# Long raw and split tiles handed out by columns, and two own buffers for the conditioning rows, in a one-core encoder layer

## The chip, the cores and the metric

One Trainium2 chip, one core. The metric is device time in microseconds (us) of one execution; lower is better. The engines are TensorE (PE, with its weight loads shown as PEld), VectorE (DVE), ScalarE (ACT), GpSimd (POOL) and SyncE (SP), which issues most of the transfers. Each engine works through its own instructions in program order, and semaphores hold an instruction back until what it needs is there.

## The reference, cut to what matters

One encoder layer on x of 1024 tokens by 1024 channels, float32, with a conditioning vector c of 1024:

```
mod = silu(c) @ w_ada + b_ada            # 6 x 1024: shift, scale and gate for two halves
h   = rms_norm(x, g1) * (1 + scale) + shift
q, k, v, gates = h @ w_in                # 20 heads, 10 units of two heads, 384 columns a unit
a = neighbourhood attention (8 heads);  b = dilated windows (12 heads, 3 dilations)
y = merge of a @ w_proj_a and b @ w_proj_b by sigmoid gates
x = x + gate * (y @ w_o)
x = x + gate2 * SwiGLU(rms_norm(x, g2) modulated by the rest of mod)
```

All of it is float32 to the precision of a split product: each operand is cut into a high part and a low part, and three matmul passes (high by high, high by low, low by high) make one product.

## The kernel before, in words

**Start (until about 60 us).** x is loaded, transposed and normed. The conditioning vector's first two blocks of columns (2 x 1024) come in eight blocks of `land` tiles (two transfers of 512 KB each), and PE multiplies them with c block by block (`ada_rows`, L789). ACT copies the row out (`rowk`, L795), PE turns it into columns (L804), DVE finishes them (`sc`, L809 and L811) and scales `yT` (L816), ACT takes the high part of h (L821), DVE the low part (L824), and ACT sends `yT` off to `h_d` (L826, issued from ACT's own queue). The first unit's weights come in between (`raw`, 192 KB for 128 x 384 columns; ACT `whi` L118, DVE `wlo` L119), and PE multiplies block after block (`start_chunk`, L834).

**Units (60 to about 525 us).** Ten units u of two heads; six are dilated, four neighbourhood. A unit has 8 steps t of 128 tokens, and a step has 8 chunks k of three 384-column matmuls each (`proj_chunk`, L312). Step n is 8u + t. Between the chunks PE does the attention of earlier units. The weights of the next unit come by `unit_load` on SP (into 6 raw buffers of 512 columns), and `wsplit` makes the high part on ACT (L118) and the low part on POOL or DVE (L119), into 10 buffers of 512 columns: k = 0 and 1 in step 6, the other six within step 7's chunks, odd k on DVE. The norm of q and k (L330 to L335), their rotation (L342 to L345), the scaling after PE's turn (L377, then L400 to L402) and the softmax rows run on ACT, DVE and POOL.

**Conditioning rows in between.** The other 4096 columns of mod are made in 64 turns of `ada_step`: eight sums (`acc`, one buffer) of eight multiply-adds each on DVE (the first of a sum is L299, the other seven L301), whose 512 columns of w_ada stand in `wa` tiles. One transfer (L283) brings two turns' worth, 512 KB, into one of 8 large buffers shared with `land`, two turns ahead. `ada_row` sums a finished `acc` over the partitions on PE (L271) and writes the row (L274 to L276).

**What sets the order.** PE's order is written by hand for the whole kernel. In the start the other engines' order is written by hand too. Behind that, a scheduler orders ACT, DVE, POOL and SP by priorities and by when it takes buffers to come free. Loads and stores are told done on eight lanes (DMAHW0 to DMAHW7) that are used in turn, and an issue on a lane waits until the earlier one there has landed.

After the units come the gates, the merges, the output projection and the feed-forward part (to 1507 us), in which PE is the limit nearly throughout.

Of the kernel before, what the change touches and what calls it, by code (L numbers as in the profile page):

```python
# [23 lines left out]
NRAW, NHL = 6, 10  # L24
# [19 lines left out]
def hybrid_layer(ctx: ExitStack, tc: tile.TileContext, x, colp, wada1, wada2, bada2, wqkv, wg, wpa, wpb,  # L44
                 wo, w1, w2, hgain, ropeg, rope, rbias, bmask, g2r, out):
    nc = tc.nc

    def pool(name, side, **kw):
        return tc.alloc_tile_pool(name=name, bufs=1, side=side, reuse_waits="tile", **kw)
# [4 lines left out]
    wp = pool("w", "left")  # L54
# [6 lines left out]
    o_d = tc.dram_tile([6, 128, S], F32, name="o_d")  # L61
# [44 lines left out]
    def fview(ap):  # L106
        return ap.bitcast(F32)

    def wload(src, n):
        raw = wp.tile([128, 512], F32, tag="raw", bufs=NRAW, name="raw")  # L110
        nc.sync.dma_start(raw[:, :n], src)
        return raw[:, :n]

    def wsplit(r, eng=None):
        n = r.shape[1]
        hi = wp.tile([128, 512], F32R, tag="hi", bufs=NHL, name="whi")
        lo = wp.tile([128, 512], F32R, tag="lo", bufs=NHL, name="wlo")
        nc.scalar.activation(hi[:, :n], r, AF.Copy)  # L118
        (eng or nc.gpsimd).tensor_sub(lo[:, :n], r, fview(hi[:, :n]))  # L119
        return hi, lo  # L120

    def wslot(src, n):
# [20 lines left out]
    ap_ = pool("attn", "right")  # L143
# [2 lines left out]
    nc.vector.memset(c32, 0.0)  # L146
    nc.vector.tensor_copy(c32[:, :, 0], cact)

    NBIG, NLAND = 8, 7

    def big(name, shape=None, dtype=F32):
        return ap_.tile(shape or wide, dtype, tag="big", bufs=NBIG, name=name)
# [1 line left out]
    yT = [ap_.tile([128, 4, S], F32, tag="qk", bufs=2, name="yT") for _ in range(2)]  # L154
    land = [big("land") for _ in range(NLAND)]
    for tag, n, bufs in (("bm", 512, 1), ("p", 512, 4), ("qn", 256, 7), ("rtab", 512, 1), ("acc2", 512, 1), ("pT", 512, 4),
                         ("stg", 512, 3), ("vs", 128, 2), ("ra", 64, 2), ("rb", 64, 2)):
        ap_.tile([128, n], F32, tag=tag, bufs=bufs, name="place")
    seq = [0]

# [19 lines left out]
    def unit_load(u, k):  # L180
        return wload(wqkv[u, :, k, :], 384)
# [85 lines left out]
    ada_acc = {}  # L267

    def ada_row(c):
        pm = bank("t")  # L270
        nc.tensor.matmul(pm[0:1, :], ones, ada_acc[c], start=True, stop=True)  # L271
        row = wp.tile([1, 512], F32, tag="raw", bufs=NRAW, name="row")
        br = wp.tile([1, 512], F32, tag="raw", bufs=NRAW, name="brow")
        nc.sync.dma_start(br, bada2[:, c * 512:(c + 1) * 512])  # L274
        nc.vector.tensor_add(row, pm[0:1, :], br)
        nc.sync.dma_start(mod_d[c * 512:(c + 1) * 512].rearrange("(o n) -> o n", o=1), row)  # L276

    def ada_load(i):

        if i < 64 and i not in ada_acc.setdefault("w", {}):  # L280
            c, kk = divmod(i, 8)
            ada_acc["w"][i] = big("wa2", [128, 2, 512])
            nc.sync.dma_start(ada_acc["w"][i], wada2[c, :, kk:kk + 2, :])  # L283

    def ada_step():
        i = ada_state["i"]
        ada_state["i"] += 1
        c, kk = divmod(i, 8)
        if kk == 0 and c > 0:
            ada_row(c - 1)  # L290
        if i >= 64:
            return
        if kk % 2 == 0:
            ada_load(i)
            ada_load(i + 2)
        wa = ada_acc["w"][i - kk % 2][:, kk % 2, :]
        if kk == 0:
            ada_acc[c] = ap_.tile([128, 512], F32, tag="acc2", bufs=1, name="acc2")
            nc.vector.tensor_scalar(ada_acc[c], wa, cact[:, 0:1], None, op0=ALU.mult)  # L299
        else:  # L300
            nc.vector.scalar_tensor_tensor(ada_acc[c], wa, cact[:, kk:kk + 1], ada_acc[c],  # L301
                                           op0=ALU.mult, op1=ALU.add)
# [222 lines left out]
    class Cluster:  # L525


        def __init__(self):
            self.items, self.keys = [], 0
# [114 lines left out]
    def combine_prep(i):  # L644
        pr, g, hf = i // 6, (i % 6) // 2, i % 2
        if g == 0 and hf == 0:
            cb["acc"] = big("oacc")
        ut = wp.tile([128, 512], F32, tag="raw", bufs=NRAW, name="ut")
        u = u_d[g * 2 + pr]
        if g == 0:  # L650
            nc.sync.dma_start(ut, u[:, hf * 512:hf * 512 + 512])
            uv = ut
        elif g == 1:
            nc.sync.dma_start(ut.rearrange("p (r i) -> p r i", r=4),
                              u.rearrange("p (r h i) -> p h r i", r=4, h=2)[:, hf])
            uv = ut.rearrange("p (r i) -> p i r", r=4)
        else:
            nc.sync.dma_start(ut.rearrange("p (t i) -> p t i", t=8),
                              u.rearrange("p (t i) -> p t i", t=8)[:, :, hf * 64:hf * 64 + 64])
            uv = ut.rearrange("p (t i) -> p i t", t=8)  # L660
        fb = wp.tile([128, 4, 2, 64], F32, tag="raw", bufs=NRAW, name="fb")
        for hd in range(2):
            nc.vector.tensor_copy(fb[:, :, hd, :], cb["fe"][:, g, hf * 4:hf * 4 + 4, pr, hd, None]
                                  .to_broadcast([128, 4, 64]))
        cb[i] = (fb, ut, uv, cb["acc"])
# [254 lines left out]
    raws = {}  # L920
    nextw = {}
    for n in range(6, 92):
        u, t = divmod(n, 8)
# [7 lines left out]
        else:  # L931
            chunks = []
        if u + 1 < 10:
            for k in ([0, 1, 2, 3, 4, 5, 6, 7] if n == 6 else [t] if u else []):
                raws[u + 1, k] = unit_load(u + 1, k)
            if t == 6:
                for k in range(2):
                    nextw[u + 1, k] = wsplit(raws[u + 1, k])
        if t == 2 and 1 <= u <= 10:
            for slot, I in unit_items(units[u - 1]):  # L940
                if I.U.kind < 3:
# [19 lines left out]
        def chunk():  # L961
            if chunks:
                chunks.pop(0)()
                k = 8 - len(chunks)
                if t == 7 and u + 1 < 10 and k < 8 and k >= 2:
                    nextw[u + 1, k] = wsplit(raws[u + 1, k], nc.vector if k % 2 else None)

        turns = [(units[0], tt) for tt in {8: (0, 1), 9: (2, 3), 11: (4, 5), 13: (6, 7)}.get(n, ())]
        if PAIRED <= n <= 81 or 9 < n < PAIRED and n % 2:
# [56 lines left out]

    def gate_mixes(i, order):
        r = {q: gate_raw(i, q) for q in (0, 2, 3, 1)}
        s1 = wp.tile([128, 512], F32, tag="raw", bufs=NRAW, name="ws")
# [103 lines left out]
    def o_split():  # L1133
        for pr in (4, 5, 0, 1, 2, 3):
            oT[pr] = ttp.tile([128, 2, S], F32R, tag="t", bufs=6, name="oT")
            for hf in range(2):
                hs = slice(hf * 512, hf * 512 + 512)
                raw = wp.tile([128, 512], F32, tag="raw", bufs=NRAW, name="raw")
                nc.sync.dma_start(raw, o_d[pr][:, hs])
# [198 lines left out]
    def late_weights(j):  # L1338
        if j in EARLY[:2]:
            n = EARLY.index(j)  # L1340
            for nm, src in (("x2", w1_d[n, 1]), ("x3", w1_d[n, 2]), ("x1", w1_d[n, 0]), ("w22", w1[j, :, 12:16, :]),
                            ("x4", w1_d[n, 3])):
                wj[j, nm] = wsplit(wload(src, 512), nc.vector if n == 0 or nm in ("x3", "w22") else None)
            return
        r = {q: wload(w1[j, :, 4 * q:4 * q + 4, :], 512) for q in (0, 2, 3, 1)}
        s1, s2 = (wp.tile([128, 512], F32, tag="raw", bufs=NRAW, name="ws") for _ in range(2))
# [12 lines left out]
        nc.gpsimd.tensor_sub(s4, r[1], s4)  # L1359
        wj[j, "x4"] = wsplit(s4, nc.vector)  # L1360
# [305 lines left out]
```

## Time and profile before

| | |
|---|---|
| Runs | 1507.0, 1508.83, 1510.0 us; median 1508.83 |
| Profiled execution | 1508.52 us; its span, first to last instruction, 1506.7 us |
| PE busy | 1485.7 us, 99% of the span, 8156 matmuls |
| DVE busy | 1090.2 us (72%) |
| ACT busy | 668.2 us (44%) |
| POOL busy | 535.1 us (36%) |
| Mean granted TensorE clock | 0.999 |
| Transfers | 241.65 MB, 160 GB/s on average; 45.7% of 16 engines' span on the main queue |

How to read it: a row of the list of operations in time gives the start, the duration, the engine, the line, the operation with its output and inputs, and in brackets the idle time before it with what ended it. "PE ps_d L312 <- DVE wlo L119" in the list of waits means that PE's matmul of line 312 stood until DVE's operation of line 119 was done; the three numbers are the total in us, the count, and the longest. Matmuls overlap, so their pace is read from start to start (0.17 us for 384 columns) and not from their durations (0.33 us). PEclk is the granted clock, 1.00 being the full one.

### The profile page before, as it was taken

What the parts mean: (1) busy time and instruction counts of PE and PEld (TensorE: products, weight loads), DVE (VectorE), ACT (ScalarE), POOL (GpSimd) and SP (SyncE); (2) the same over time, 40 slices, a digit from 0 to 9 for tenths busy, and PEclk for the clock granted to TensorE, in tenths of its full rate; (3) what the DMA queues carried; (4) which work ended last, traced back from release to release, by engine and by line L of the source; (5) the groups of instructions that cost most, each with busy time, mean ns of one, the idle gap of its engine ahead of it and who ended that gap; (6) DMA issues with size and microseconds to landing.
All of it is one profiled execution on the core that took longest, in us unless ns stands there. A gap on an engine that the chain in (4) does not pass through costs nothing. (4 is left out here: it accounts for less than half of the span.)

```text
span 1506.7 us, 24201 instructions
## 1 busy us (share of the span) xinstructions
PE 1485.7 (99%) x8156; PEld 1265.1 (84%) x8156; DVE 1090.2 (72%) x2265; ACT 668.2 (44%) x1691; POOL 535.1 (36%) x540
## 2 busy tenths in 40 slices
PE   9999999999999999999999999999999999999998
PEld 7998989998888877788888888888888888887886
DVE  6867767767889845367675597788767777599468
ACT  5555655555645554246432354233223323354442
POOL 0432332321100040002352301676767776104464
PEclk9999999999999999999999999999999999999999
DMA  9625445645245164824553225345433334898342
GB/s 373 236 85 179 144 132 162 196 139 166 61 131 168 45 197 143 327 85 128 161 195 137 90 90 181 126 127 181 155 125 109 108 106 144 278 372 281 98 153 100
DMA packets 150637, 241.65 MB, mean 160 GB/s; under 512 B 26464, under 2 KB 69088, under 8 KB 149744
## 3 DMA queue, kind: packets, MB, share of 16 engines
q1 hardware_dynamic: 131936, 226.45, 45.7%
q10 hardware_dynamic: 18576, 13.64, 2.8%
q8 instruction: 65, 1.06, 0.3%
q14 instruction: 60, 0.49, 0.1%
HBM read 179.89 MB, written 60.15 MB: 159 GB/s over the span
## 5 line engine op out<-in xcount | busy, mean ns | idle before, releaser
L119 POOL TENSOR_TENSOR wlo<-raw,whi 128x512 fp32r<-128x512 f32 (+2 forms) x133 | 172.9, 1314 | 461.7 <-ACT whi L118 287.0
L118 ACT ACTIVATE whi<-raw 128x512 fp32r<-128x512 f32 (+1 forms) x348 | 203.6, 599 | 252.4 <-PE ps_s L1501 42.3
L312 PE MATMUL ps_d<-whi,hT 128*128 128x384 f32 x1152 | 310.8, 341 | 0.0
L119 DVE TENSOR_TENSOR wlo<-raw,whi 128x512 fp32r<-128x512 f32 (+1 forms) x215 | 183.6, 867 | 76.8 <-ACT whi L118 72.4
L312 PEld LDWEIGHTS ps_d<-whi,hT 128*128 128x128 f32 x1152 | 209.9, 188 | 5.2 <-ACT vs L350 3.5
L312 PE MATMUL ps_d<-wlo,hT 128*128 128x384 f32 x576 | 193.6, 336 | 2.9 <-DVE wlo L119 2.7
L312 PEld LDWEIGHTS ps_d<-wlo,hT 128*128 128x128 f32 x576 | 108.7, 189 | 4.0 <-DVE wlo L119 3.4
L118 ACT ACTIVATE whi<-ws 128x512 fp32r<-128x512 f32 x65 | 40.8, 628 | 126.9 <-DVE ws L1348 79.8
L1281 POOL TENSOR_TENSOR e<-e,c 128x512 f32<-128x512 f32 x44 | 68.9, 1565 | 59.2 <-DVE c L1411 35.0
L342 POOL TENSOR_TENSOR ra<-qn,rtab 128x64 f32<-128x64 f32 x48 | 16.3, 340 | 156.7 <-DVE qn L335 105.8
L119 POOL TENSOR_TENSOR wlo<-m,whi 128x512 fp32r<-128x512 f32 x35 | 51.4, 1479 | 54.5 <-ACT whi L118 54.5
L1279 ACT ACTIVATE e<-e 128x512 f32<-128x512 f32 x44 | 27.5, 631 | 95.1 <-DVE e L1414 66.4
L555 ACT ACTIVATE P<-P,st 128x256 f32<-128x256 f32 (+2 forms) x100 | 45.8, 460 | 41.4 <-DVE st L553 41.3
L712 PE MATMUL ps_d<-hT,whi 128*128 128x512 f32 x192 | 60.6, 397 | 0.0
L1331 PE MATMUL ps_v<-h2T,whi 128*128 128x512 f32 x192 | 59.2, 389 | 0.0
L1331 PE MATMUL ps_s<-h2T,whi 128*128 128x512 f32 x192 | 59.1, 389 | 0.0
L129 ACT ACTIVATE ry<-ss,eps 128x4 f32<-128x4 f32 (+1 forms) x88 | 26.2, 298 | 70.1 <-DVE ss L333 56.7
L1331 PE MATMUL ps_d<-h2T,whi 128*128 128x512 f32 x184 | 56.8, 390 | 0.0
L491 ACT ACTIVATE P<-P,sx 128x384 f32<-128x384 f32 (+1 forms) x64 | 37.1, 580 | 43.6 <-DVE sx L490 43.4
L119 DVE TENSOR_TENSOR wlo<-ws,whi 128x512 fp32r<-128x512 f32 x45 | 49.7, 1105 | 8.0 <-ACT whi L118 7.8
L1280 DVE TENSOR_TENSOR e<-e 128x512 f32<-128x512 f32 x44 | 42.5, 973 | 17.8 <-ACT e L1279 17.7
L301 DVE SCALAR_TENSOR_TENSOR acc<-wa,cact,acc 128x512 f32<-128x512 f32 x56 | 42.6, 762 | 16.8 <-DMA wa<-in_wada_dram 16.5
(445 smaller groups left out, 3956.8 us busy)
## 6 DMA issues: line engine op xcount, KB each, us to landing
raw<-in_w_dram SPq DMA_DIRECT2D x139, 256.0 KB
ga_d<-e SPq DMA_DIRECT2D x77, 256.0 KB
raw<-ga_d SPq DMA_DIRECT2D x77, 256.0 KB
wa<-in_wada_dram SPq DMA_DIRECT2D x32, 512.0 KB
raw<-in_wqkv_dram SPq DMA_DIRECT2D x80, 192.0 KB
m<-in_w_dram SPq DMA_DIRECT2D x44, 256.0 KB
raw<-in_wg_dram SPq DMA_DIRECT2D x42, 256.0 KB
xt<-in_x_dram SPq DMA_DIRECT2D x16, 512.0 KB
```

The costliest lines, as they stand in the source:

```text
L118: nc.scalar.activation(hi[:, :n], r, AF.Copy)
L119: (eng or nc.gpsimd).tensor_sub(lo[:, :n], r, fview(hi[:, :n]))
L129: nc.scalar.activation(y, ss, AF.Ln, scale=1.0 / n, bias=eps)
L301: nc.vector.scalar_tensor_tensor(ada_acc[c], wa, cact[:, kk:kk + 1], ada_acc[c], op0=ALU.mult, op1=ALU.add)
L312: nc.tensor.matmul(pd[:, :384], tok(a, k, t), U.w[k][b][:, :384], start=(k == 0 and i == 0), stop=(k == KT - 1 and i == 2))
L491: nc.scalar.activation(P[:nq, :nk], P[:nq, :nk], AF.Exp, scale=-1.0, bias=nm, accum_out=sm)
L555: nc.scalar.activation(C.P[h][:nq, c], C.P[h][:nq, c], AF.Exp, scale=-1.0, bias=nm, accum_out=sm)
L712: nc.tensor.matmul(st["p"], gw[i, br][j][a][:, kk * 128:(kk + 1) * 128], hT[b][:, k, hs], start=(k == 0 and q == 0), stop=(k == 7 and q == 2))
L1279: nc.scalar.activation(sg, a, AF.Sigmoid)
L1280: nc.vector.tensor_mul(sg, sg, a)
L1281: nc.gpsimd.tensor_mul(sg, sg, up)
L1331: nc.tensor.matmul(pb, w[p][:, k * 128:(k + 1) * 128], b[q][:, k], start=(k == 0 and i == 0), stop=(k == 3 and i == 2))
```

## The change

- **Ring.** The raw tile is one long tile of 3072 columns, and the high and low parts are two long tiles of 5120 columns. A `take(n)` hands out the next n columns and wraps round at the end. Unit weights take 384 columns each, so there are 8 raw slots and 13 slots for the parts, in the same memory that held 6 and 10 of 512. Elsewhere 512 columns are taken, on a multiple of 512, which gives 6 and 10 as before.
- **When weights are loaded and split.** From unit 1 on, the raws of the next unit are loaded one per step (two in step 6), and written as split one per step: k = 0 to 4 in steps 2 to 6, k = 5 to 7 behind the first three chunks of step 7. k = 1, 3 and 6 are on DVE.
- **Conditioning rows.** `wa` has two buffers of its own of 128 x 512. Each of the 64 turns has a transfer of 256 KB of its own, issued one turn ahead. The large buffers are 7 instead of 8. The row and its bias share one large buffer instead of two raw ones.
- `fb`, which held a raw buffer, takes one of the three `stg` buffers; `ut` and the feed-forward's sums take from the ring.

```
+    class Ring:
+        def __init__(self, n, dtype, name):
+            self.t, self.n, self.at = wp.tile([128, n], dtype, name=name), n, 0
+        def take(self, n, packed=False):
+            if n == 512 and not packed:
+                self.at = -(-self.at // 512) * 512
+            if self.at + n > self.n:
+                self.at = 0
+            self.at += n
+            return self.t[:, self.at - n:self.at]
+    rawr = Ring(NRAW * 512, F32, "raw")
+    hir, lor = Ring(NHL * 512, F32R, "whi"), Ring(NHL * 512, F32R, "wlo")
...
-    NBIG, NLAND = 8, 7
+    NBIG, NLAND = 7, 7
...
-            ada_acc["w"][i] = big("wa2", [128, 2, 512])
-            nc.sync.dma_start(ada_acc["w"][i], wada2[c, :, kk:kk + 2, :])
+            ada_acc["w"][i] = ap_.tile([128, 512], F32, tag="wa", bufs=2, name="wa2")
+            nc.sync.dma_start(ada_acc["w"][i], wada2[c, :, kk, :])
...
-        if kk % 2 == 0:
-            ada_load(i)
-            ada_load(i + 2)
-        wa = ada_acc["w"][i - kk % 2][:, kk % 2, :]
+        ada_load(i)
+        ada_load(i + 1)
+        wa = ada_acc["w"][i]
...
-        fb = wp.tile([128, 4, 2, 64], F32, tag="raw", bufs=NRAW, name="fb")
+        fb = ap_.tile([128, 4, 2, 64], F32, tag="stg", bufs=3, name="fb")
...
         if u + 1 < 10:
-            for k in ([0, 1, 2, 3, 4, 5, 6, 7] if n == 6 else [t] if u else []):
+            for k in (t - 2,) if 2 <= t < 7 and u else ():
+                nextw[u + 1, k] = wsplit(raws[u + 1, k], nc.vector if k in (1, 3) else None)
+            for k in range(5) if n == 6 else range(5, 8) if n == 7 else (6, 7) if t == 6 else (t,) if t < 6 else ():
                 raws[u + 1, k] = unit_load(u + 1, k)
-            if t == 6:
-                for k in range(2):
-                    nextw[u + 1, k] = wsplit(raws[u + 1, k])
+            for k in range(5) if n == 6 else ():
+                nextw[u + 1, k] = wsplit(raws[u + 1, k], nc.vector if k in (1, 3) else None)
...
-                if t == 7 and u + 1 < 10 and k < 8 and k >= 2:
-                    nextw[u + 1, k] = wsplit(raws[u + 1, k], nc.vector if k % 2 else None)
+                if t == 7 and u + 1 < 10 and k <= 3:
+                    nextw[u + 1, k + 4] = wsplit(raws[u + 1, k + 4], nc.vector if k == 2 else None)
```

The number of compute instructions is the same, and PE's rows are in the same order, one for one. SP has 32 rows more. Line numbers after the ring are higher by 15 or 16: L118 and L119 are now L134 and L135, L178 is L194, L283 is L299, L299 and L301 are L314 and L316, L826 is L841.

**SP in the start, behind the sixth `land` transfer.** `land` is half a block of conditioning columns, `raw` the first unit's weights, `wa_` the conditioning rows of the 64 turns. Before:

```order
L178 DMA land<-in_wada_dram 128x1024 [waits DMAHW5_49]
L178 DMA land<-in_wada_dram 128x1024 [waits DMAHW6_49,PE_49]
L111 DMA raw<-in_wqkv_dram 128x384 [waits DMAHW7_49]
L178 DMA land<-in_wada_dram 128x1024 [waits DMAHW0_49,PE_49]
L178 DMA land<-in_wada_dram 128x1024 [waits DMAHW1_49,PE_49]
L111 DMA raw<-in_wqkv_dram 128x384 [waits DMAHW2_49]
```

These are block 3's two halves, the fourth raw, block 4's two halves and the fifth raw. After, on the same engine and place:

```order
L194 DMA land<-in_wada_dram 128x1024 [waits DMAHW5_49]
L299 DMA wa_1057<-in_wada_dram 128x512 [waits DMAHW6_49]
L299 DMA wa_1059<-in_wada_dram 128x512 [waits DMAHW7_49]
L194 DMA land<-in_wada_dram 128x1024 [waits DMAHW0_49,PE_49]
L128 DMA raw<-in_wqkv_dram 128x384 [waits DMAHW1_49]
L194 DMA land<-in_wada_dram 128x1024 [waits DMAHW2_49,PE_49]
L194 DMA land<-in_wada_dram 128x1024 [waits DMAHW3_49,PE_49]
```

Two loads of conditioning rows, whose buffers are free from the beginning, now stand between the halves of block 3. Each later transfer here is on another lane than before.

**ACT and DVE in the start, at the second block of h.** ACT's rows before, from the first store of `yT` on:

```order
L826 DMA h_d<-yT 128x1024 [waits DMAHW7_49]
L118 ACTIVATE whi<-raw 128x384
L821 ACTIVATE hT_112<-yT 128x512 [waits DVE_49] x2
L826 DMA h_d<-yT 128x1024 [waits DMAHW1_49]
L795 ACTIVATE rowk<-ps_t 128x256 [waits PE_49]
```

ACT's rows after:

```order
L841 DMA h_d<-yT 128x1024 [waits DMAHW2_49]
L134 ACTIVATE whi<-raw 128x384 [waits DMAHW7_49]
L836 ACTIVATE hT_115<-yT 128x512 [waits DVE_49] x2
L841 DMA h_d<-yT 128x1024 [waits DMAHW4_49]
L810 ACTIVATE rowk<-ps_t 128x256 [waits PE_49]
```

The rows are the same, but the first store waits for the lane on which block 4's first half was put (before, the lane of the fourth raw). DVE's rows after, at the same block:

```order
L831 TENSOR_SCALAR yT<-yT,sc 128x512 [waits DVE_49]
L831 TENSOR_SCALAR yT<-yT,sc 128x512
L135 TENSOR_TENSOR wlo<-raw,whi 128x384 [waits DMAHW7_49,Activation_49]
L314 TENSOR_SCALAR acc_1061<-wa_1057,cact 128x512 [waits DMAHW6_49]
L839 TENSOR_TENSOR hT_405<-yT,hT_115 128x512 [waits Activation_49] x2
```

The row of `acc` between `wlo` and `hT` was not there before; the other four were. Six of the first sum's eight turns now stand in the start.

**DVE where unit 4 begins.** `tp` is a sum or difference of blocks of h that the gates will use later, `qk` the scaled and turned q and k, `wlo` a low part of weights. Before:

```order
L753 TENSOR_TENSOR tp<-tp 128x2x256 [waits DMAHW3_49,DMAHW2_49]
L754 TENSOR_TENSOR tp<-tp 128x256 [waits DVE_49]
L755 TENSOR_TENSOR tp<-tp 128x256 [waits DVE_49]
L401 SCALAR_TENSOR_TENSOR qk<-ps_v,hg,qk 128x4x64 [waits Activation_49]
L402 TENSOR_TENSOR qk<-ps_v,qk 128x4x64
L119 TENSOR_TENSOR wlo<-raw,whi 128x384 [waits DMAHW1_49,Activation_49]
```

After:

```order
L568 ISA P,st<-ps_s,bmask 128x256 [waits PE_49]
L568 ISA st 128x1
L350 TENSOR_TENSOR qn<-qn,ry 128x256 [waits DVE_49,Pool_49]
L568 ISA P,st<-ps_s,bmask 128x256
L568 ISA st 128x1
L590 COPY PT<-ps_t 128x512 [waits PE_49]
L416 SCALAR_TENSOR_TENSOR qk<-ps_v,hg,qk 128x4x64 [waits Activation_49]
L417 TENSOR_TENSOR qk<-ps_v,qk 128x4x64
L135 TENSOR_TENSOR wlo<-raw,whi 128x384 [waits Activation_49] x2
```

The three `tp` rows stand some thirty rows earlier, and two low parts follow `qk` where one did. All eight splits that a unit's time holds still stand in its step 7; of these, before, one or two were for the unit after next, and now four or five are.

More of the change, by code (lines that the diff above doesn't have):

```diff
@@ L107, in fview @@
         return ap.bitcast(F32)
+    class Ring:
[10 more added lines that the diff above has]
+    hir, lor = Ring(NHL * 512, F32R, "whi"), Ring(NHL * 512, F32R, "wlo")
     def wload(src, n):
-        raw = wp.tile([128, 512], F32, tag="raw", bufs=NRAW, name="raw")
-        nc.sync.dma_start(raw[:, :n], src)
-        return raw[:, :n]
+        raw = rawr.take(n if n == 384 else 512)[:, :n]
+        nc.sync.dma_start(raw, src)
+        return raw
     def wsplit(r, eng=None):
         n = r.shape[1]
[L116 to L119, printed above, removed]
+        hi, lo = (z.take(n if n == 384 else 512)[:, :n] for z in (hir, lor))
+        nc.scalar.activation(hi, r, AF.Copy)
+        (eng or nc.gpsimd).tensor_sub(lo, r, fview(hi))
         return hi, lo
@@ L156, in hybrid_layer @@
     for tag, n, bufs in (("bm", 512, 1), ("p", 512, 4), ("qn", 256, 7), ("rtab", 512, 1), ("acc2", 512, 1), ("pT", 512, 4),
-                         ("stg", 512, 3), ("vs", 128, 2), ("ra", 64, 2), ("rb", 64, 2)):
+                         ("stg", 512, 3), ("wa", 512, 2), ("vs", 128, 2), ("ra", 64, 2), ("rb", 64, 2)):
         ap_.tile([128, n], F32, tag=tag, bufs=bufs, name="place")
@@ L271, in ada_row @@
         nc.tensor.matmul(pm[0:1, :], ones, ada_acc[c], start=True, stop=True)
-        row = wp.tile([1, 512], F32, tag="raw", bufs=NRAW, name="row")
-        br = wp.tile([1, 512], F32, tag="raw", bufs=NRAW, name="brow")
+        z = big("row", [1, S])
+        row, br = z[:, 0:512], z[:, 512:1024]
         nc.sync.dma_start(br, bada2[:, c * 512:(c + 1) * 512])
@@ L647, in combine_prep @@
             cb["acc"] = big("oacc")
-        ut = wp.tile([128, 512], F32, tag="raw", bufs=NRAW, name="ut")
+        ut = rawr.take(512, True)
         u = u_d[g * 2 + pr]
@@ L1028, in gate_mixes @@
         r = {q: gate_raw(i, q) for q in (0, 2, 3, 1)}
-        s1 = wp.tile([128, 512], F32, tag="raw", bufs=NRAW, name="ws")
+        s1 = rawr.take(512)
         nc.vector.tensor_sub(r[0], r[0], r[2])
@@ L1137, in o_split @@
                 hs = slice(hf * 512, hf * 512 + 512)
-                raw = wp.tile([128, 512], F32, tag="raw", bufs=NRAW, name="raw")
-                nc.sync.dma_start(raw, o_d[pr][:, hs])
+                raw = wload(o_d[pr][:, hs], 512)
                 hi, lo = (oT[pr][:, b, hs] for b in range(2))
@@ L1345, in late_weights @@
         r = {q: wload(w1[j, :, 4 * q:4 * q + 4, :], 512) for q in (0, 2, 3, 1)}
-        s1, s2 = (wp.tile([128, 512], F32, tag="raw", bufs=NRAW, name="ws") for _ in range(2))
+        s1, s2 = rawr.take(512), rawr.take(512)
         nc.vector.tensor_add(s1, r[2], r[3])
```

## The prediction

> **What bounds the kernel now.** I read the page first, then what TensorE waited for, then the granted clock by stretches, and last the rows in time around the places that the change touches.
>
> ```profile
> span 1506.7 us, 24201 instructions
> PE 1485.7 (99%) x8156; PEld 1265.1 (84%) x8156; DVE 1090.2 (72%) x2265; ACT 668.2 (44%) x1691; POOL 535.1 (36%) x540
> ```
>
> TensorE is the bound: it stands idle for 1506.7 - 1485.7 = 21.0 us of the span, and since its own rows are the same, one for one, before and after, the change can win at most those 21 us and what a slow clock costs. So every part has to be priced in TensorE's waits. From the list of waits on TensorE, the two that name a split weight of the units:
>
> ```profile
> PE ps_d L312 <- DVE wlo L119: 2.7, 1, 2.7
> PE ps_d L312 <- POOL wlo L119: 0.2, 1, 0.2
> ```
>
> Nine unit boundaries, and only one long wait. Here it is in time, VectorE's rows and then TensorE's, and the stretches around it with the granted clock (the column behind POOL):
>
> ```profile
> 210.70 1.46 DVE L753 TENSOR_TENSOR tp<-tp 128x512 f32<-128x512 f32 x1 [2.05 <-DMA tp<-h_d]
> ...
> 214.77 0.41 DVE L402 TENSOR_TENSOR qk<-ps_v,qk 128x256 fp32r<-128x256 f32 x1
> 215.10 0.54 DVE L119 TENSOR_TENSOR wlo<-raw,whi 128x384 fp32r<-128x384 f32 x1
> ```
>
> ```profile
> 215.70 0.45 PE L312 MATMUL ps_d<-wlo,hT 128*128 128x384 f32 x1 [2.67 <-DVE wlo L119]
> ...
> 219.18 0.52 PE L312 MATMUL ps_d<-whi,hT 128*128 128x384 f32 x1
> 219.63 1.20 PE L543 MATMUL ps_s<-qk 64*128 64x256 f32 x12
> ```
>
> ```profile
> 205.00:215.00 10.00, 8.02 (x58) 7.53 (x56) 7.85 (x19) 6.00 (x19) 5.21 (x8) 1.00 0.65 204
> 215.00:220.00 5.00, 4.30 (x16) 3.87 (x18) 3.34 (x14) 1.72 (x7) 1.63 (x7) 0.67 0.22 66
> 220.00:225.00 5.00, 5.00 (x51) 4.69 (x50) 2.81 (x11) 3.67 (x13) 0.50 (x2) 0.99 0.11 27
> ```
>
> VectorE stood 2.05 us for a transfer of `tp`, did its `tp` rows, and only then the low part that TensorE needed at 213.0. Behind the wait the clock was granted at 0.67, and 14 matmuls took 219.63 - 215.70 = 3.93 us, where 14 at 0.173 us (the pace from start to start elsewhere in this loop) take 2.42: another 1.5 us.
>
> The second group are the waits for the conditioning rows. From VectorE's waits between 60 and 520 us, then five of the eight in time, and the TensorE rows that stand a little later:
>
> ```profile
> DVE acc L301 <- DMA wa<-in_wada_dram: 16.5, 8, 4.4
> ```
>
> ```profile
> 81.66 0.75 DVE L301 SCALAR_TENSOR_TENSOR acc<-wa,cact,acc 128x512 f32<-128x512 f32 x1 [1.47 <-DMA wa<-in_wada_dram]
> ...
> 140.89 0.75 DVE L301 SCALAR_TENSOR_TENSOR acc<-wa,cact,acc 128x512 f32<-128x512 f32 x1 [1.53 <-DMA wa<-in_wada_dram]
> ...
> 322.38 0.75 DVE L301 SCALAR_TENSOR_TENSOR acc<-wa,cact,acc 128x512 f32<-128x512 f32 x1 [4.36 <-DMA wa<-in_wada_dram]
> ...
> 367.13 0.75 DVE L301 SCALAR_TENSOR_TENSOR acc<-wa,cact,acc 128x512 f32<-128x512 f32 x1 [2.78 <-DMA wa<-in_wada_dram]
> ...
> 418.31 0.75 DVE L301 SCALAR_TENSOR_TENSOR acc<-wa,cact,acc 128x512 f32<-128x512 f32 x1 [3.41 <-DMA wa<-in_wada_dram]
> ```
>
> ```profile
> 86.14 0.44 PE L377 MATMUL ps_v<-ident,qn 128*128 128x128 f32 x2 [1.22 <-DVE rz L132]
> ...
> 146.00 0.44 PE L377 MATMUL ps_v<-ident,qn 128*128 128x128 f32 x2 [1.30 <-POOL qn L345]
> ...
> 369.02 0.50 PE L476 MATMUL ps_s<-qk 64*128 64x256 f32 x4 [0.95 <-DVE qk L402]
> ...
> 421.14 0.66 PE L672 MATMUL ps_t<-ident,fb 128*128 128x128 f32 x4 [0.98 <-DVE PT L506]
> ```
>
> No TensorE row names `wa`, but VectorE's loss of 1.5 to 3.4 us comes 2 to 5 us before four of TensorE's waits; that the one causes the other is my reading. The longest of all, 4.36 us at 322, is followed by none. TensorE lost 1.22 + 1.30 + 0.95 + 0.98 = 4.45 us for 16.5 us of VectorE: 0.27 us for each.
>
> **The change part by part.** The sum is against the profiled execution, 1508.52 us, which is 0.3 below the median of the runs.
>
> *Splits five chunks ahead.* All eight splits of a unit's time still stand in its step 7, so no work moves off that step: the same eight ACT and eight VectorE or GpSimd operations, 0.5 us each. What moves is for whom they are: only k = 5 to 7 are now for the unit that begins next, and the others have a unit's time. The low part at 215.10 was k = 3, so TensorE doesn't wait for it, and the three `tp` rows are out of its way as well. That takes off 2.67 + 0.2 + 1.5 = 4.4 us. Nothing less than the wait is likely, nothing more than all of it possible. What is late next is k = 5, needed 15 matmuls (2.6 us) into the unit. The splits that now have time still stand ahead of other VectorE work, as they did.
>
> On the clock, the 2.67 us wait is the longest in the attention part. [...] The trace puts the slow stretch right behind a wait of 2.67 us, so I go by the trace.
>
> *Conditioning rows, half a transfer at a time.* Six of the first sum's eight turns move into the start, and the wait at 81.66 with TensorE's at 86.14 goes with them. The rest are 256 KB each through two buffers: load i+2 is issued when turn i is done. The trace has no such load; the nearest rows are a weight load of the same size, issued by SP and waited for by ACT, and a conditioning load of 512 KB (317.80, used at 322.38, 4.6 us):
>
> ```profile
> 698.36 0.33 SPq L111 DMA_DIRECT2D raw<-in_wpa_dram  x1
> ...
> 701.49 0.63 ACT L118 ACTIVATE whi<-raw 128x512 fp32r<-128x512 f32 x1 [3.33 <-DMA raw<-in_wpa_dram]
> ```
>
> ```profile
> 317.80 0.85 SPq L283 DMA_DIRECT2D wa<-in_wada_dram  x2
> ```
>
> So a round trip is 3.1 us (701.49 - 698.36) and about 0.4 for SP's issue, 3.5 in all. In VectorE's new order I counted the rows between turn i and turn i+2. In most pairs there are nine or more, at 1090.2 / 2265 = 0.48 us each, which covers it. In seven pairs there are four or five (1.9 or 2.4 us): late by 1.6 twice and by 1.1 five times, 8.7 us, and 0.8 from shorter ones. That is 9.5 us of VectorE's time where there were 16.5; by 0.27 it costs TensorE 2.6 us where 4.45 stood: 1.9 off. The bounds: none of the new waits reaches TensorE (4.45 off), or each does in full because VectorE is nearly full where the last ones are (54.40 of 60 us here), 9.5 - 4.45 = 5 on top:
>
> ```profile
> 460.00:520.00 60.00, 58.24 (x424) 50.16 (x420) 54.40 (x177) 31.07 (x110) 5.11 (x4) 1.00 0.38 118
> ```
>
> [...]
>
> *The start.* Here transfers are the limit:
>
> ```profile
> 24.00:32.00 8.00, 7.63 (x58) 6.01 (x58) 6.01 (x15) 3.53 (x8) 0.00 (x0) 1.00 1.03 414
> ```
>
> At 414 GB/s the two `wa` loads put in front of block 3's second half hold up everything behind by 524288 B / 414 GB/s = 1.27 us. The rows of TensorE, ACT and VectorE where that arrives:
>
> ```profile
> 27.08 1.34 PE L789 MATMUL ps_t<-land,c 128*32 128x256 f32 x16 [0.29 <-DVE sc L811]
> ...
> 30.45 0.62 PE L834 MATMUL ps_d<-whi,hT 128*128 128x384 f32 x2
> ```
>
> ```profile
> 28.23 0.35 ACTq L826 DMA_DIRECT2D h_d<-yT  x1
> 28.62 0.53 ACT L118 ACTIVATE whi<-raw 128x384 fp32r<-128x384 f32 x1 [2.52 <-DMA raw<-in_wqkv_dram]
> ...
> 30.68 0.33 ACTq L826 DMA_DIRECT2D h_d<-yT  x1
> ```
>
> ```profile
> 29.18 0.56 DVE L119 TENSOR_TENSOR wlo<-raw,whi 128x384 fp32r<-128x384 f32 x1 [1.12 <-ACT whi L118]
> 29.71 1.29 DVE L824 TENSOR_TENSOR hT<-yT,hT 128x512 fp32r<-128x512 f32 x2
> ```
>
> ```profile
> L299 DVE TENSOR_SCALAR acc<-wa,cact x8: 464/466/560, 61.5 to 473.4; 128x512 f32<-128x512 f32 x8
> ```
>
> ACT's first store of `yT` waits at 28.23 for its lane, the fourth raw's. The second waits until 30.68 for the lane of block 4's second half; block 4's first half is one 512 KB transfer sooner, about 29.4. In the new order the first store waits for that first half, and the two `wa` loads are ahead of it: 29.4 + 1.27 = 30.7, 2.4 us later than 28.23. The high part of the second block's weights, its low part, then the new `acc` row (0.47) and `hT` follow on: 2.4 + 0.47 = 2.9 us. TensorE's matmul at 30.45 is held by just that `hT`, whose first row ends at about 30.4, so it has no slack: +2.85. TensorE's order is fixed and later blocks run behind, so it isn't won back. Block 3's own wait (1.27 at 27.08) lies inside this. The bounds: 1.27, if the lane isn't the last to come, and 4, if the third block is held by its lane too, one 512 KB (1.27) later.
>
> *At nothing:* the ring itself (the same operations in the same memory), raws earlier (SP), `fb` in `stg`, the row in a large buffer (`row` and its bias are waited for by one TensorE row of 1.1 us). The cover is VectorE's free quarter in the middle; without it, 0 to 1 us.
>
> Sum: -4.4 - 1.9 + 2.85 = -3.45, 1508.52 - 3.45 = 1505.07 for such an execution, 1505.4 against the median.
>
> **The rivals.** *The start's delay is hidden.* Store and lane don't bind, or TensorE catches up in later stalls of the start. For it: TensorE idles 60 - 56.71 = 3.3 us of the first 60. Against it: no row of slack at 30.45. Then -6.3: 1502.5.
>
> *Slower: the two buffers.* VectorE is in order, so a late `wa` holds all that stands behind it, and SP's next issues stand behind a load that waits for its buffer. 42 loads depend on a turn two before. Should each be late by x us, TensorE pays 42 x 0.27 x against the 4.45 that go: even with the other terms (-4.4 + 2.85 = -1.55) the sum is zero at x = 6.0 / 11.3 = 0.53 us. At 1.2 us late it is 13.6 - 6.0 = +7.6: 1516. For it: the two-turn gap of four or five rows in the seven pairs. Against it: most gaps are nine rows and more, and 512 KB with two loads ahead were late in only 8 of 32.
>
> *The change doesn't do what it says.* Splits aren't one per step but all in step 7, and some other low part (k = 5 on GpSimd, whose operation takes over 1 us) holds TensorE at a boundary instead. Then -4.4 goes to about 0 and the sum is -1.9 + 2.85 = +1: 1509.8, no change that can be told.
>
> **How the numbers follow.** A difference under 0.2% (3.0 us, about what a measurement of this kernel tells from none) counts as the same: 1505.8 to 1511.8. Chances: my forecast 0.38, and it lies 0.4 us inside faster, so I give 0.22 of it to faster and 0.16 to same; the hidden start 0.22, faster; the splits not helping 0.19, same; the two buffers 0.21, slower in nearly all. Together faster 0.44, same 0.36, slower 0.20. The range holds the forecast with its bounds, the hidden start down to 1500.8 (with all of 4.45 off: 1502.5 - 2.6 = 1499.9 at the very end), and of the slower case the part up to x = 0.85: 1501 to 1512.5.
>
> **What would show it.** At about 215 us no wait of TensorE on `wlo`, and a clock of 1.00 throughout 210 to 225. VectorE's waits on `wa` near 9.5 us in all instead of 16.5, in waits of 1 to 2 us, at turns that follow closely. In the start, ACT's first store of `yT` at about 30.7 instead of 28.2, and the matmul now at 30.45 at about 33.3. Wrong it would be if that matmul stays within 1 us of 30.5, if the `wa` waits exceed 20 us, or if TensorE waits for k = 5 to 7 at several boundaries.

## The result and the profile after

The changed kernel is slower: 1549.49 us in the median of 4 runs (1544.82 to 1550.77), against 1508.2 for the kernel before. The ratio is 1.0267, 95% interval 1.0242 to 1.0292. 1505.4 was forecast, and the range ended at 1512.5.

The page of the changed kernel, span and engines:

```profile
span 1548.5 us, 24211 instructions
PE 1501.3 (97%) x8156; PEld 1275.6 (82%) x8156; DVE 1079.9 (70%) x2265; ACT 666.1 (43%) x1691; POOL 544.8 (35%) x540
```

TensorE ran the same 8156 matmuls. Its busy time rose from 1485.7 to 1501.3 us (15.6 more, and the mean granted clock fell from 0.999 to 0.989), its idle time from 21.0 to 47.2 (26.2 more). So of the 41.8 us by which the span grew, five eighths are waits and three eighths are the same matmuls at a slower clock. The list of TensorE's waits, its first five rows:

```profile
PE ps_d L1516 <- DVE wlo L135: 6.6, 5, 3.2
PE ps_t L517 <- ACT PT L523: 6.0, 2, 4.8
PE ps_v L392 <- DVE rz L148: 5.9, 2, 3.8
PE ps_d L327 <- ACT vs L365: 4.8, 6, 1.6
PE ps_v L1346 <- ACT whi L134: 3.5, 1, 3.5
```

Two of these rows (L1346 and L1516) belong to the feed-forward part, which the prediction does not mention at all. The wait of L327 (L312 before) for a low part, `wlo`, is not in the whole list any more.

Since TensorE's order is the same row for row, the start of each of its matmuls can be set against that of the same matmul before. This gives what is lost (or, with a minus, gained) in each stretch, in us. The stretches are cut by the time of the kernel before, and each line is one profiled execution (that of e3 is its slowest, 4.7 us above its median):

| kernel | start, to 60 | units, 60 to 600 | 600 to 1050 | feed-forward 1, to 1300 | feed-forward 2, to the end | sum |
|---|---|---|---|---|---|---|
| changed kernel | 5.9 | 16.3 | 0.7 | 9.8 | 9.2 | 41.8 |
| e1 ring alone, 512 wide | 1.2 | (4.5) | -0.2 | 7.6 | 7.0 | 20.0 |
| e2 own rows alone | 4.1 | 6.7 | 0.1 | 0.0 | 0.2 | 11.1 |
| e3 changed, rows as before | 1.6 | 4.8 | 0.0 | 8.1 | 12.2 | 26.7 |
| e4 changed, slots in freed order | 4.4 | 11.6 | 0.8 | 0.0 | 8.2 | 25.0 |
| e5 slots and split times, raw in pool | 1.0 | -2.4 | -0.6 | 0.0 | 4.0 | 2.0 |
| e6 own rows, none in the start | 2.0 | 7.0 | 0.1 | 0.0 | -0.6 | 8.6 |
| e7 slots, old split times, raw in pool | 0.4 | -6.0 | 1.3 | 0.0 | 6.3 | 2.0 |
| e8 changed, rows and times as before | 2.3 | (0.2) | -0.1 | 8.8 | 10.2 | 21.3 |
| e9 is e7 with ACT's order kept | 1.2 | -8.0 | 1.3 | 0.0 | 0.1 | -5.5 |
| e10 is e5 with ACT's order kept | 1.0 | -3.2 | 0.9 | 0.0 | 0.1 | -1.2 |
| e11 own rows, two loads in all | 3.2 | 4.4 | 0.6 | 0.0 | -0.6 | 7.7 |
| e12 changed, raw in pool | 6.0 | 8.5 | 1.6 | 0.0 | 2.8 | 19.0 |

The changed kernel and e4 have the same rows on every engine in the units, and still differ by 4.7 there and by 1.5 in the start, so these columns are good to about that. Much of it is the clock: behind the same wait of TensorE (at 317.84 in the one, 314.0 in the other) the granted clock was 0.54 over 7 us in the changed kernel and 0.78 in e4. In e1 and e8 some of the unit weights' raws are overwritten before they are split (six slots for eight raws in the one, `ut` passing the ring on in the other), so their units are set in brackets and not used.

### The profile page after: what moved, and what is told of

Its sections match the earlier page's. It is cut to its first block, busy times and chain, and to the rows that moved or that the text cites. A ratio compares the mean times of both kernels' runs of the same rounds, so it can differ in the third digit from the quotient of the medians.

```text
span 1548.5 us, 24211 instructions
## 1 busy us (share of the span) xinstructions
PE 1501.3 (97%) x8156; PEld 1275.6 (82%) x8156; DVE 1079.9 (70%) x2265; ACT 666.1 (43%) x1691; POOL 544.8 (35%) x540
## 5 line engine op out<-in xcount | busy, mean ns | idle before, releaser
L134 ACT ACTIVATE whi<-raw 128x512 fp32r<-128x512 f32 (+2 forms) x413 | 238.8, 602 | 377.2 <-DVE raw L1363 101.3
L135 POOL TENSOR_TENSOR wlo<-raw,whi 128x512 fp32r<-128x512 f32 (+2 forms) x153 | 203.1, 1338 | 535.4 <-ACT whi L134 492.8
L327 PE MATMUL ps_d<-whi,hT 128*128 128x384 f32 x1152 | 314.9, 344 | 4.8 <-ACT vs L365 4.8
L135 DVE TENSOR_TENSOR wlo<-raw,whi 128x512 fp32r<-128x512 f32 (+1 forms) x260 | 212.7, 829 | 94.4 <-ACT whi L134 91.3
L327 PEld LDWEIGHTS ps_d<-whi,hT 128*128 128x128 f32 x1152 | 212.6, 191 | 11.8 <-ACT vs L365 10.0
L327 PE MATMUL ps_d<-wlo,hT 128*128 128x384 f32 x576 | 194.7, 338 | 0.0
L327 PEld LDWEIGHTS ps_d<-wlo,hT 128*128 128x128 f32 x576 | 110.1, 191 | 0.0
L1294 ACT ACTIVATE e<-e 128x512 f32<-128x512 f32 x44 | 27.5, 632 | 124.8 <-DVE e L1429 66.9
L135 POOL TENSOR_TENSOR wlo<-m,whi 128x512 fp32r<-128x512 f32 x35 | 48.6, 1390 | 63.1 <-ACT whi L134 63.1
L1295 DVE TENSOR_TENSOR e<-e 128x512 f32<-128x512 f32 x44 | 49.1, 1117 | 18.0 <-ACT e L1294 18.0
L1346 PE MATMUL ps_v<-h2T,whi 128*128 128x512 f32 x192 | 59.2, 389 | 0.0
L1346 PE MATMUL ps_s<-h2T,whi 128*128 128x512 f32 x192 | 59.1, 389 | 0.0
L145 ACT ACTIVATE ry<-ss,eps 128x4 f32<-128x4 f32 (+1 forms) x88 | 26.2, 298 | 73.6 <-DVE ss L348 63.6
L1346 PE MATMUL ps_d<-h2T,whi 128*128 128x512 f32 x184 | 56.7, 390 | 0.0
L1362 DVE TENSOR_TENSOR raw<-raw 128x512 f32<-128x512 f32 x20 | 14.5, 723 | 60.6 <-DMA raw<-in_w_dram 56.8
L316 DVE SCALAR_TENSOR_TENSOR acc<-wa,cact,acc 128x512 f32<-128x512 f32 x56 | 43.3, 773 | 17.6 <-DMA wa<-in_wada_dram 17.5
L505 DVE CUSTOM_DVE_ANT_0 P<-ps_s,rb 128x384 f32<-128x384 f32 (+1 forms) x64 | 31.4, 519 | 25.4 <-PE ps_s L491 25.3
```

The lines of the kernel that those rows point to most:

```text
L134: nc.scalar.activation(hi, r, AF.Copy)
L135: (eng or nc.gpsimd).tensor_sub(lo, r, fview(hi))
L327: nc.tensor.matmul(pd[:, :384], tok(a, k, t), U.w[k][b][:, :384], start=(k == 0 and i == 0), stop=(k == KT - 1 and i == 2))
L505: nc.vector.tensor_tensor_reduce(P[:nq, :nk], pS[:nq, :nk], I.masks[h], -1.0, 3.0e38, ALU.add, ALU.min, nm)
L1295: nc.vector.tensor_mul(sg, sg, a)
L1346: nc.tensor.matmul(pb, w[p][:, k * 128:(k + 1) * 128], b[q][:, k], start=(k == 0 and i == 0), stop=(k == 3 and i == 2))
```

## The experiments

**Which part costs it.** "Own rows" stands for the two own buffers of the conditioning rows, and "split times" for when the weights are loaded and split. e1 undoes everything but the ring, e2 everything but the own rows, e3 only the own rows, e8 the own rows and the split times. Lines left out of the code are marked by `...`.

```
e1   raw, whi, wlo: Ring, always take(512); all else as before
e2   before, with
-            ada_acc["w"][i] = big("wa2", [128, 2, 512])
+            ada_acc["w"][i] = ap_.tile([128, 512], F32, tag="wa", bufs=2, name="wa2")
...
e3   changed, with the - line of e2, NBIG 8, two turns a load
e8   e3 with the old split times
```

> Before, with nothing but the long tiles handed out by columns, always 512 wide: 6 raw slots and 10 for the parts, taken in turn; split times, conditioning rows and all else as before. Theory A (three separate costs: the fixed turn of raw slots in the feed-forward part, the conditioning rows' own buffers, a small gain from the splits): the 20 us that the changed kernel loses behind 1050 us are all here, VectorE's waits of the feed-forward's sums on raw loads are near 47 us as in the changed kernel (1.6 before), and the time is 1508 + 20 = 1528, with little lost ahead of 1050. Theory B (one cost, the conditioning rows' loads, whose lateness shifts all that follows): no loss here, 1508 within 3.

Measured: 1528.45 us, ratio 1.0139 (1.0124 to 1.0154). 14.6 of its 20.0 us are lost behind 1050 us, where theory A put all 20; that the time fits so well is in part luck.

> Before, with nothing but the conditioning rows changed: two buffers of their own of 256 KB, one load a turn, 7 large buffers, the row and its bias in a large one. Theory A: about 5 us lost in the start and 10 to 15 in the units, nothing behind 1050: 1523 to 1528. Theory B: most of the whole loss, 1540 or more.

Measured: 1518.94 us, 1.0085 (1.0062 to 1.0107): 4.1 in the start, 6.7 in the units (theory A said 10 to 15), nothing behind.

> The changed kernel with the conditioning rows loaded as before (512 KB for two turns, in 8 large buffers); ring, 13 slots and split times as changed. Theory A: the 20 us behind 1050 stay, the start's 5.7 and most of the units' loss go, and the wait at unit 4's begin is gone: 1508 + 20 - 4 = 1524. Theory B: faster than before, about 1504.

Measured: 1531.59 us, 1.0161 (1.0137 to 1.0185); 20.3 behind 1050 us, the start mostly back, but the units still 4.8 slower, so 1531.59 instead of theory A's 1524.

> The changed kernel with conditioning rows and split times of before: what is left of the change is the ring for all three tiles, with 8 raw slots and 13 for the parts. Theory A2: behind 1050 us the same 17 to 20 us as in the other kernels with a raw ring; in the units 0 to 6 lost by the raw slots' fixed turn; 1525 to 1532. Theory B2 (split times): the units lose nothing here: 1525.

Measured: 1529.89 us, 1.0155 (1.0130 to 1.0179), 19.0 us lost behind 1050. Theory B, one cause, is out: the ring costs most behind 1050, the own rows ahead of it.

**Why the ring costs the feed-forward part.** VectorE's waits behind 1050 us, before, changed, and e12 (where the raw tiles stay in their pool); `ws` and, in the ring, `raw` of L1362 is the first of two sums of weights:

```profile
DVE ws L1347 <- POOL wlo L119: 23.4, 8, 5.4
...
DVE ws L1347 <- DMA raw<-in_w_dram: 1.6, 1, 1.6
```

```profile
DVE raw L1362 <- DMA raw<-in_w_dram: 46.7, 12, 6.4
```

```profile
DVE ws L1362 <- POOL wlo L134: 23.0, 8, 5.3
...
DVE ws L1362 <- DMA raw<-in_w_dram: 2.8, 2, 1.5
```

Each line of waits gives the total in us, the count and the longest. With the pool the sum waits mostly for GpSimd's `wlo`, which by my reading (not shown) holds the buffer that the sum is to take. With the ring it waits for its operands. VectorE's order differs there too; the same stretch of it, before (from 1072.91 us) and changed (from 1107.90 us):

```
c<-c,ps_s  e<-e,ps_s  c<-c,ps_t  ws<-raw    e<-e,ps_v  wlo<-ws  ws<-ws,raw  e<-e
c<-c,ps_s  e<-e,ps_s  c<-c,ps_t  e<-e,ps_v  wlo<-raw   raw<-raw  e<-e       raw<-raw
```

And on TensorE, in the changed kernel, at another such item, whose sum (1101.79) had waited 2.81 us for its load:

```profile
1101.71 0.39 PE L1346 MATMUL ps_t<-h2T,wlo 128*128 128x512 f32 x1
1105.62 0.76 PE L1346 MATMUL ps_v<-t,whi 128*128 128x512 f32 x1 [3.53 <-ACT whi L134]
```

In e4 the six slots go to the next item in the order in which this one frees them, r0, r2, s1, r3, r1, s2 (the turn would be r0, r2, r3, r1, s1, s2):

```
...
+        r = {q: six[n] for n, q in enumerate((0, 2, 3, 1))}
+        s1, s2 = six[4:]
+        six[:] = [r[0], r[2], s1, r[3], r[1], s2]
...
```

> The changed kernel, but the six raw slots of the feed-forward's first part are handed out in the order in which the item before frees them, not in turn. Theory A: VectorE's sums no longer stand for loads there (47 us to under 10), and the 9 us that TensorE loses between 1050 and 1250 come back: about 1540. Theory B, or the fixed turn not being the cause: no change, 1549.

Measured: 1536.23 us, 1.0197 (1.0180 to 1.0215), and 0.0 lost between 1050 and 1300, where the changed kernel lost 9.8. So the slots' order is the cause there. Behind 1300 e4 still loses 8.2. What the raw ring costs there and in the units (6.4 and 7.8 by the changed kernel against e12) is not traced to one cause. The expectation that the sums' waits fall under 10 us missed: they still wait for loads, but half as long, and never over 2.6 us:

```profile
DVE raw L1369 <- DMA raw<-in_w_dram: 23.9, 12, 2.6
```

**What is left without the raw ring.** e5 keeps the 13 slots for the parts and the new split times, and leaves the raw tiles in the pool and the rows as before; e7 has the old split times besides.

```
+    hir, lor = Ring(NHL * 512, F32R, "whi"), Ring(NHL * 512, F32R, "wlo")
...
         raw = wp.tile([128, 512], F32, tag="raw", bufs=NRAW, name="raw")
```

> Before, with the change's 13 slots for the high and low parts and its split times, but the raw tiles left in their pool of 6 buffers and the conditioning rows as before. Theory A2 (the loss is the raw tiles' fixed turn, behind 1050 us and partly in the units, and the conditioning rows' own buffers): nothing lost in the feed-forward part, the wait at unit 4's begin gone (-4), 1508 - 4 = 1504, at most 1508. Theory B2 (the new split times push VectorE's and ACT's other work late in the units, as the 5 us lost at 369 and later in the changed kernel with its rows undone may show): 1509 to 1513.

Measured: 1511.77 us, 1.0039 (1.0025 to 1.0053): in the range of theory B2, but not where it said, since the units won 2.4 us.

> The kernel of the run with raw tiles in their pool and 13 slots, but with the split times of before. Theory A2: the wait at unit 4's begin depends on the order of VectorE's rows there, which any change moves, so it is gone here too in half of the cases; 1504 to 1508. Theory C (splits five ahead are what removes it): it stays, 1508.

Measured: 1510.89 us, 1.0026 (1.0012 to 1.0040), outside both ranges. Theory C falls all the same: the wait at unit 4's begin is gone with the old split times too. Both kernels win in the units and lose 4 to 6 us in the feed-forward's second part, where ACT's rows and then TensorE's in e7 are these:

```profile
1372.46 0.63 ACT L133 ACTIVATE whi<-m 128x512 fp32r<-128x512 f32 x1 [1.10 <-PE ps_s L1516]
1373.84 0.63 ACT L133 ACTIVATE whi<-raw 128x512 fp32r<-128x512 f32 x1 [0.74 <-DMA raw<-ga_d]
1375.18 0.63 ACT L133 ACTIVATE whi<-m 128x512 fp32r<-128x512 f32 x1 [0.72 <-PE ps_s L1516]
```

```profile
1376.39 0.49 PE L1516 MATMUL ps_d<-whi 128*128 128x512 f32 x1 [1.24 <-ACT whi L133]
1378.18 0.80 PE L1516 MATMUL ps_d<-wlo,whi 128*128 128x512 f32 x1 [1.30 <-DVE wlo L134]
1378.77 0.63 PE L1516 MATMUL ps_d<-whi,wlo 128*128 128x512 f32 x1
```

The splits of `m`, the fourth product's, stand ahead of the third product's last `raw` and wait there for TensorE to free a slot; TensorE waits for that `raw`. In the kernel before, seven splits of `raw` (1370.32 to 1378.71) come ahead of the first of `m`. e9 and e10 are e7 and e5 with ACT's splits of these two products kept in the order of the code:

```
...
-        return wsplit(a, nc.vector), wsplit(b, ...)
+        keep = pin if n in (2, 3) else lambda x: x
+        return wsplit(a, nc.vector, keep), wsplit(b, ..., keep)
```

> The kernel with 13 slots for the high and low parts, the split times of before and the raw tiles in their pool, and besides the high parts of the third and fourth product of the feed-forward's second part kept in the order in which they are written, which gives ACT and VectorE the rows of before there, one for one. Theory D (the fixed turn lets ACT's splits for the fourth product, whose inputs are on the chip early, stand ahead of the third's last ones and wait there for TensorE to free their slots; this costs the 6 us at 1370 to 1385): they come back, 1511 - 6 = 1505, faster than before by 1 to 5. Rival (TensorE's waits there come from VectorE's contention, not from the order): no change, 1511.

Measured: 1504.16 us, 0.9979 (0.9966 to 0.9992). The 6.3 us are back to 0.1. This version is 0.2% faster than the kernel before: TensorE busy 1484.6 of a span of 1501.3.

> The same with the change's split times. Theory D: 4 us back, 1507 to 1508, the same as before: the new split times themselves win nothing, since the wait at unit 4's begin is gone with the old times too. Rival (the split times win 3 to 4 us): 1503.

Measured: 1508.63 us, 1.0003 (0.9993 to 1.0013), about as expected: against e9, the new split times give back what the 13 slots win. Two other pairs show less of it, e5 against e7 (2 us) and e3 against e8 (1 us), both within their noise.

**The conditioning rows.**

> Before, with the conditioning rows' own two buffers alone, and these buffers held by two rows of the start (blocks 6 and 7 of its conditioning product, taken from the pool of four before) until the start's end, so that no such load can go out in the start. Theory A2: the 4.1 us of the start (a land transfer 1.3 us late, and the slow clock behind that wait) go, and the loads pile up later: the units lose 7 as before or up to 3 more, 1515 to 1518 against 1519 of the own buffers alone. Rival: the start's loss is only moved (the loads still cost their 1.5 MB of transfer time ahead of what TensorE needs): 1519.

```
+            tag, bufs = ("wa", 2) if k >= 6 else ("p", 4)
```

Measured: 1515.68 us, 1.0058 (1.0044 to 1.0073); 2.0 lost in the start where e2 lost 4.1. By these two executions the loads in the start cost about half of that; the rest is not settled.

> Before with the conditioning rows' own two buffers, but only the first two of the 64 loads are made, and all turns use these two tiles (the rows are then not those of the reference). Theory A2 (the 7 us in the units are VectorE's waits for loads that a turn two before holds up): VectorE waits for no such load, the 7 us go and the 4.45 us of TensorE that the old waits cost go too: the start's 4 stay, 1508 + 4 - 4 - 4 = 1504. Rival (the order of VectorE's rows, which the two buffers make, costs it, not the waits): 1515 to 1519.

```
-        if i < 64 and i not in ada_acc.setdefault("w", {}):
+        if i < 2 and i not in ada_acc.setdefault("w", {}):
...
+        wa = ada_acc["w"][i % 2]
```

Measured: 1518.29 us, 1.0068 (1.0050 to 1.0086). Theory A2 falls. VectorE can't wait for `wa` at all here, and the units lose 4.4 us all the same. VectorE's waits of the units in e2, and then in e11:

```profile
DVE ss L332 <- ACT sq L329: 19.7, 23, 2.0
...
DVE acc L300 <- DMA wa<-in_wada_dram: 13.8, 18, 3.7
```

```profile
DVE ss L332 <- ACT sq L329: 29.9, 30, 2.2
```

Take 13.8 us of one wait away, and another grows by 10.2 us. The intervals of e2 and e11 overlap, so what the waits on `wa` cost TensorE can't be told from nothing. What in the new order of VectorE, ACT and SP costs the 4.4 us stays open; e11 has an order of its own, which leaves that of e2 within the start.

> The whole change except that the raw tiles (with the row, fb and the sums) stay in the pool of 6 buffers; the conditioning rows have their own two buffers, the parts 13 slots, and the split times are the changed kernel's. By the runs so far, stage by stage as TensorE's delay against before: start 4 (own rows), units -2 from slots and split times, +7 from own rows, +5 at 1370 to 1390. Theory E (the parts add up unless raw ring and own rows meet): units +5, 1508 + 14 = 1522, and the 4.8 us wait of TensorE near 497, which only the kernels with both show, is not there. Rival (split times and own rows are what meet, without the raw ring): units +10 or more, 1527 or more.

Measured: 1529.02 us, 1.0152 (1.0130 to 1.0173), between the two theories (units 8.5). The 4.8 us wait near 497 is gone, as theory E said; in the changed kernel ACT stood there for a gate weight's raw, which SP had issued between two loads of `wa`:

```profile
494.22 0.63 ACT L134 ACTIVATE whi<-raw 128x512 fp32r<-128x512 f32 x1 [5.47 <-DMA raw<-in_wg_dram]
```

```profile
496.88 0.90 PE L517 MATMUL ps_t<-ident,P 128*128 128x128 f32 x3 [4.78 <-ACT PT L523]
```

**The sum, step by step**, from the ratios (0.1% is 1.5 us): 13 slots with ACT's order kept -3 (e9), new split times +4 (e10 over e9), ACT's order not kept +5 (e5 over e10), own rows +17 (e12 over e5), raw ring +17 (changed over e12): 40, which is the loss. By the intervals of the ratios I estimate each step to be good to 2 to 5 us. The steps hold along this path: the own rows alone cost 13 (e2), and 16 on top of the whole ring (changed over e3).

## Why the prediction was wrong

**"At nothing: the ring itself (the same operations in the same memory)" was the step that failed most**: with the raw ring 17 us, and 5 more by ACT's order in the second feed-forward part. The operations and the memory are the same. What isn't is which buffer a load gets and what may stand ahead of what. Where the slots go to the next item in the order in which they come free (e4), the 9.8 us of the first feed-forward part are gone; where they go by turn, they are lost. The prediction looked at VectorE's, ACT's and SP's order in the start and the units and took the rest as the same.

**The start, +2.85, was 5.9, and not by the chain that was forecast.** ACT's first store of `yT` was forecast at 30.7 and came at 32.15, and the low part of `hT` behind it at 33.98. The matmul that was forecast at 33.3 came at 35.14. But the store did not hold it: TensorE waits for nothing between block 3's wait and this matmul.

```profile
30.45 1.08 PE L804 MATMUL ps_t<-land,c 128*32 128x256 f32 x8 [2.00 <-DMA land<-in_wada_dram]
...
34.50 0.52 PE L849 MATMUL ps_d<-whi,hT 128*128 128x384 f32 x1
34.82 0.52 PE L849 MATMUL ps_d<-wlo,hT 128*128 128x384 f32 x1
35.14 0.84 PE L849 MATMUL ps_d<-whi,hT 128*128 128x384 f32 x2
```

```profile
32.15 0.35 ACTq L841 DMA_DIRECT2D h_d<-yT  x1
32.55 0.52 ACT L134 ACTIVATE whi<-raw 128x384 fp32r<-128x384 f32 x1 [5.71 <-DMA land<-in_wada_dram]
```

```profile
33.98 1.29 DVE L839 TENSOR_TENSOR hT<-yT,hT 128x512 fp32r<-128x512 f32 x2
```

Block 3's wait, put at 1.27 and inside the other, was 2.00, and behind it the granted clock was 0.52 instead of 1.00:

```profile
20.00:30.00 10.00, 8.03 (x81) 5.70 (x77) 6.46 (x15) 4.67 (x10) 0.00 (x0) 1.00 1.04 407
30.00:37.00 7.00, 6.55 (x26) 5.75 (x27) 3.90 (x10) 2.75 (x6) 0.00 (x0) 0.52 1.02 373
37.00:60.00 23.00, 22.75 (x177) 20.04 (x176) 18.74 (x40) 11.08 (x25) 7.27 (x7) 1.00 1.00 371
```

So it was the other way round: the chain lay inside block 3's wait and its slow clock, if not by much (the first of these two `hT` rows ends at about 34.6, half a microsecond ahead of the matmul, and in e11 and e12 TensorE waits 0.2 to 0.3 us for `hT`). Matmuls 0.32 us apart instead of 0.17 took TensorE from 3.1 us late (28.34 before, 31.45 now) to 5.3 late (31.80 and 37.12). The prediction counted the waits' slow clock as a gain at 215 us and as a loss nowhere.

**Splits, -4.4: right in size, wrong in cause.** The wait on the low part is gone and so is its slow clock (1.00 from 205 to 225 us in the changed kernel, where 215 to 220 had 0.67 before). But e7 and e9, with the old split times, have none either. What goes with it are the 13 slots: none of the nine kernels that have them shows a wait of TensorE on `wlo` between 60 and 600 us, whatever the split times. The kernels with the old 10 buffers all have such waits, at other places. In e2 unit 4's begin has 0.6 us of them left, but the units have 3.0 us in all, as much as before (2.7 and 0.2):

```profile
PE ps_d L311 <- DVE wlo L119: 1.6, 1, 1.6
PE ps_d L311 <- POOL wlo L119: 1.4, 3, 0.6
```

e7 differs from the kernel before by these slots alone. The new split times by themselves cost up to 4 us (e10 over e9).

**Conditioning rows, -1.9: wrong.** The round trip was about right (3.5 us in the median from issue to landing; 3.1 and 0.4 for the issue were assumed). VectorE's waits on `wa` came to 17.5 us in 18 places instead of 9.5: rows between two turns were priced at the mean 0.48 us, and several there are of 0.16. One stretch of VectorE in the changed kernel:

```profile
311.44 0.74 DVE L316 SCALAR_TENSOR_TENSOR acc<-wa,cact,acc 128x512 f32<-128x512 f32 x1
312.10 0.16 DVE L146 TENSOR_SCALAR rv<-ss 128x4 f32<-128x4 f32 x1
312.36 0.16 DVE L148 TENSOR_TENSOR rz<-ry,rv 128x4 f32<-128x4 f32 x1
312.56 0.16 DVE L149 SCALAR_TENSOR_TENSOR rz<-rz,ry 128x4 f32<-128x4 f32 x1
314.06 0.75 DVE L316 SCALAR_TENSOR_TENSOR acc<-wa,cact,acc 128x512 f32<-128x512 f32 x1 [1.35 <-DMA wa<-in_wada_dram]
```

```profile
316.20 0.99 POOL L135 TENSOR_TENSOR wlo<-raw,whi 128x384 fp32r<-128x384 f32 x1
317.16 0.63 POOL L360 TENSOR_TENSOR qn<-ra,rb 128x64 f32<-128x64 f32 x1
```

`ry` (L150) stands behind the waiting row; `qn`, which is made from it, ends on GpSimd at 317.79, and TensorE's wait for `qn` until 317.84 was 3.83 us, the longest of its kind (the list of waits puts it down to `rz`, which ends at the same time). But of these 3.83 the wait on `wa` is 1.35, and a split that stands ahead of `qn` on GpSimd another 0.99. And the price of 0.27 us for each us of VectorE, which rested on four waits that lay near in time, doesn't hold: e11 has none of these waits and loses most of it. Together with the start, the own rows were to cost 0.95 us and cost 13 alone (e2). The rival with the two buffers named the side and, as 1516, about what e2 shows (1518.94), but in part by luck: its mechanism is at most about a third of the loss in the units (6.7 in e2, 4.4 in e11 without it).

## What to carry to other kernels

Replacing a pool by slots in a fixed turn is not free when the operations stay the same (17 us here for the raw tiles): look at every engine's order through the whole program, not only at the places that the change is about, and at which buffer a load waits for. A wait that is gone from its place may stand at others, so add up all waits of its kind, and undo the parts of a change one by one before naming the part that cured it. A chain that comes late has cost nothing until the limiting engine is seen to wait for it: look at that engine's own rows first. When an engine's wait is removed and the time stays, that wait was not the price; leaving the loads out altogether told that in one run.

## What the runs showed of the hardware

TensorE's waits can cost more than themselves: in the changed kernel 26.2 us of new waits came with 15.6 us of slower clock (0.989 in the mean instead of 0.999). In e11, 6.5 us more idle time than before (27.5) came with almost none (1.1 us more busy time, clock 0.999). Waits of 1.33 us (e2, at 29.34, granted clock 0.50 from 29.4 to 32), 2.00 us (0.52 from 30 to 37) and 3.83 us (0.54 from 317 to 324) all had a slow clock behind them. In the changed kernel the matmuls of 384 columns stood there at 0.32 us from start to start instead of 0.17. The first row is e2's, the second the changed kernel's:

```profile
29.40:32.00 2.60, 2.60 (x13) 1.79 (x14) 1.27 (x3) 1.56 (x3) 0.00 (x0) 0.50 1.05 419
```

```profile
317.00:324.00 7.00, 6.16 (x24) 6.17 (x25) 5.63 (x17) 4.95 (x18) 4.11 (x9) 0.54 0.54 147
```

In shorter stretches the slow clock reads 0.50: from 30 to 36 and from 317 to 323 us in the changed kernel, and from 217 to 220 in the kernel before. Not each such wait has it: behind the kernel before's wait of 1.74 us, which ends at 1361.39, longer than e2's of 1.33, the granted clock was 1.00:

```profile
1361.00:1366.00 5.00, 4.61 (x20) 3.85 (x21) 5.00 (x9) 1.59 (x3) 0.00 (x0) 1.00 0.86 274
```
